# One-hot rows of a gate matrix: weight and comparison in one step on VectorE or ScalarE

## The chip, the cores and the metric

The kernel runs on one core of a Trainium2 chip. The time is the device time of one execution of the whole program, in microseconds (us). Before the change the median of three runs was 4549.05 us (4546.78 to 4557.33); the execution that was profiled took 4552.61 us.

## The reference

One layer of a hybrid decoder step for 512 prompt tokens and 32 sample tokens (544 in all, model width 2048). The part that matters here is its last one, the PEER channel mixer: every token picks, for 8 heads, 16 of 16384 one-neuron experts, and gets

```
e   = chosen expert ids (i1 * 128 + i2), 8 heads x 16 per token
g   = softmax(scores of the chosen)
act = gelu(peer_u[e] . x)
out = sum over the chosen of  g * act * peer_v[e]
```

So each token has 128 pairs (expert id, weight). The ids split into a row number i1 and a column number i2, both from 0 to 127.

## The kernel before

The 544 tokens are computed in two ways. 192 of them gather their expert rows one by one with indirect DMAs (the "rows" of line 1081, 384 of them, multiplied into accumulators on VectorE at lines 1129 and 1137). These run in the background, each tied to a matmul of the foreground by a dependency, so that they keep the pace of TensorE. The other 352 tokens take the dense way: TensorE multiplies all 16384 experts with the 352 tokens (`up`, 128 blocks of 128 experts), the result goes through gelu and is multiplied with a dense gate matrix G[expert, token], which is zero nearly everywhere; `down` multiplies that with all of `peer_v`.

`gate_matrix` (lines 1206 to 1255) builds G. It runs as a background task beside some 22 of the `up` blocks in the foreground. The tokens come in 4 tiles of up to 128; for each tile, three 128x128 matrices (i1, i2 and the weights) are transposed on TensorE and copied out of PSUM by ScalarE (lines 1218 to 1223; tiles `Ti1`, `Ti2`, `Tgv`, printed as `Ti` and `Tgv`). After that a partition is one of the 128 picks of a token, and a column is a token. Then, for four tokens at a time (a "quad", 88 in all, 8 to a group of 32 tokens):

- line 1244: VectorE makes `o2`, the one-hot of i2: a 128x512 comparison of a row of 0..127 with the column of each token, spread out;
- line 1246: VectorE makes `o1`, the one-hot of i1, in the same way;
- line 1247: GpSimd multiplies `o1` by the weights;
- line 1234 (`products`, two quads later): TensorE multiplies `o2` and `o1` token by token into one PSUM bank, which is the 128x128 gate matrix of each of the four tokens;
- line 1235: ScalarE copies the bank into `gs`, 32 tokens of which are written to DRAM by line 1255.

The foreground shares these engines. For every half of an `up` block (a "stream", 1024 columns of weights, 24 matmuls of line 258) ScalarE casts the weights to a rounded high part (`hi`, line 219) and VectorE subtracts it to get the low part (`lo`, line 220); at the end of a block VectorE scales the result (line 1198) and ScalarE applies gelu (line 1199).

What sets the order: every engine works its own list in order, and the lists are fixed when the program is built. Background tasks advance by one `yield` at a time; here by 2.8 steps per stream (`bg2.rate = 2.8`, line 1275). Casts and subtractions of the streams have a higher priority. Buffers limit the run ahead: 3 of `o1`, 3 of `o2`, 2 PSUM banks for the products, 3 of `hi` and `lo`.

Of the kernel before, what the change touches and what calls it, by code (L numbers as in the profile page):

```python
# [8 lines left out]
F = mybir.dt.float32  # L9
# [3 lines left out]
AF = mybir.ActivationFunctionType  # L13
OP = mybir.AluOpType
# [159 lines left out]
def program(tc, ins, outs):  # L174
    nc = tc.nc
    es = ExitStack()

    def pool(name, stack, bufs=1, **k):
        if k.get("space") is None:
            k["reuse_waits"] = "tile"  # L180
        return stack.enter_context(tc.tile_pool(name=name, bufs=bufs, **k))
# [20 lines left out]
    iota = cst[:, C_IOTA:C_IOTA + 128]  # L202
# [110 lines left out]
    p = ps_w.tile([128, 512], F, name="w1")  # L313
# [25 lines left out]
    for c in range(0, 8, 2):  # L339
        bg.rate = 1.6 if c > 2 else 0.4  # L340
        p = ps_mm.tile([128, 2, 512], F, name="mm")
# [6 lines left out]
    for ch in range(2):  # L348
        p = ps_mm.tile([128, 2, 512], F, name="mm")
# [23 lines left out]
    bias = [caus] + [ap.tile([128, (qb + 1) * 128], F, name=f"bias{qb}") for qb in range(1, 4)]  # L373
# [149 lines left out]
    for qb in range(1, 4):  # L523
        p = ps_w.tile([128, 512], F, name="w1")
# [4 lines left out]
    p = ps_w.tile([128, 512], F, name="w1")  # L529
# [94 lines left out]
    for n in range(2):  # L624
        s = staged(CH_V + n)
        p = ps_w.tile([128, 512], F, name="w1")
# [3 lines left out]
        p = ps_w.tile([128, 512], F, name="w1")  # L630
# [575 lines left out]
    def gate_matrix(t, groups, g0):  # L1206

        e1 = ra.tile([128, 128], I32, name="e1")
        nc.vector.tensor_copy(e1, ev[:, t])
        nc.vector.tensor_scalar(e1, e1, 7, None, op0=OP.arith_shift_right)  # L1210
        f1 = ra.tile([128, 128], F, name="f1")
        nc.vector.tensor_copy(f1, e1)
        f2 = ra.tile([128, 128], F, name="f2")
        nc.vector.scalar_tensor_tensor(f2, f1, -128.0, ev[:, t], op0=OP.mult, op1=OP.add)
        yield
        yield
        tr = []
        for nm, src in (("i1", f1), ("i2", f2), ("gv", gw[:, t])):
            p = ps_w.tile([128, 512], F, name="w1")
            nc.tensor.transpose(p[:, :128], src, ident)  # L1220
            d_ = ra.tile([128, 128], F, name="T" + nm)
            nc.scalar.copy(d_, p[:, :128])
            tr.append(d_)
        yield
        yield

        def wide(v, tk):
            return v[:, tk:tk + 4, None].to_broadcast([128, 4, 128])

        io = iota[:, None, :].to_broadcast([128, 4, 128])  # L1230
        def products(gs, q, o1, o2):
            p = ps_w.tile([128, 512], F, name="w1")
            for j in range(4):
                nc.tensor.matmul(p[:, j * 128:(j + 1) * 128], o2[:, j], o1[:, j], start=True, stop=True)
            nc.scalar.copy(gs[:, :, q * 4:q * 4 + 4].rearrange("p i t -> p t i"),
                           p.rearrange("p (t i) -> p t i", t=4))

        for i, tg in enumerate(groups):
            gs = ra.tile([128, 128, 32], F, name="gs", bufs=2)
            waiting = []  # L1240
            for q in range(8):
                tk = tg * 32 + q * 4
                o2 = ra.tile([128, 4, 128], F, name="o2", bufs=3)
                nc.vector.tensor_tensor(o2, io, wide(tr[1], tk), op=OP.is_equal)
                o1 = ra.tile([128, 4, 128], F, name="o1", bufs=3)
                nc.vector.tensor_tensor(o1, io, wide(tr[0], tk), op=OP.is_equal)
                nc.gpsimd.tensor_tensor(o1, o1, wide(tr[2], tk), op=OP.mult)
                waiting.append((q, o1, o2))
                if len(waiting) > 2:
                    products(gs, *waiting.pop(0))  # L1250
                yield
            for w in waiting:
                products(gs, *w)
                yield
            nc.sync.dma_start(g_dram[g0 + i], gs)
# [9 lines left out]
    while bg.queue:  # L1265
# [5 lines left out]
    ra = pool("ra", ras)  # L1271
    n1 = N1 // 32
    bg2.add(gate_matrix(1, range(4 - n1, 4), 0), gate_matrix(2, range(4), n1), gate_matrix(3, range(4), n1 + 4),
            gate_matrix(4, (0,), n1 + 8))
    bg2.rate = 2.8
    bg3.rate = 0.3
# [114 lines left out]
```

## Time and profile before

| | before |
|---|---|
| median of 3 runs | 4549.05 us |
| profiled execution | 4552.61 us |
| its span in the trace | 4550.8 us |
| TensorE busy | 4336.5 us (95%) |
| VectorE busy | 3281.7 us (72%) |
| ScalarE busy | 1728.2 us (38%) |
| GpSimd busy | 1277.5 us (28%) |

The profile shows one execution. PE is TensorE (PEld its weight load), DVE is VectorE, ACT is ScalarE, POOL is GpSimd, SP the engine that issues most DMAs. A busy share is an average over stages that differ: the gate matrix is built in one stretch of 278 us, from 2521.7 to 2799.5 us, and what counts for the change is read there. Busy time is the union of the instructions' times; instructions of one engine overlap at their ends, so what one costs its engine is the distance from its start to the next one's start, which is shorter than its duration.

### The profile page before, as it was taken

The page shows a single profiled execution, that of the slowest core. Times are in us where ns is not written, and L with a number is a line of the kernel's source. Part 1 is how long each engine was busy: PE and PEld are TensorE (multiplying, and loading weights), DVE is VectorE, ACT ScalarE, POOL GpSimd, SP SyncE. Part 2 cuts the span into 40 slices and gives each one's busy share as a digit, 9 for nine tenths or more (in the row PEclk, how much of TensorE's full clock was granted, in tenths as well). Part 3 has the DMA queues.
Part 4 walks back from the last instruction along what each step waited for, and adds up shares of the span by engine and source line. Part 5 has one row for each costly group of instructions (what it writes and reads, how often), then busy time and mean ns, then how long its engine had stood idle before and what let it go on. Part 6 is the DMA issues. An engine that isn't in the chain of part 4 may idle for free. (4 is left out here: it accounts for less than half of the span.)

```text
span 4550.8 us, 73815 instructions
## 1 busy us (share of the span) xinstructions
PE 4336.5 (95%) x29249; PEld 4147.9 (91%) x29249; DVE 3281.7 (72%) x4788; ACT 1728.2 (38%) x2374; POOL 1277.5 (28%) x1160
## 2 busy tenths in 40 slices
PE   8999989999999999999989899899999999999998
PEld 7976878699999889998988899898999999999998
DVE  6334735344556877778788997788888886888886
ACT  6232227454344434344323554322333333333333
POOL 3001011400001332333233563232343321343323
PEclk9999999999999999999999999999999999999999
DMA  8423443356657559989755567888999988999994
GB/s 267 165 85 115 142 131 109 118 159 185 185 177 213 161 181 333 326 317 320 255 171 173 197 234 281 318 325 323 338 336 345 352 312 276 348 346 348 346 352 167
DMA packets 342442, 1118.53 MB, mean 246 GB/s; under 512 B 42640, under 2 KB 137744, under 8 KB 289360
## 3 DMA queue, kind: packets, MB, share of 16 engines
q1 hardware_dynamic: 282704, 700.65, 46.1%
q0 software_dynamic: 59392, 413.17, 24.5%
q8 instruction: 229, 3.75, 0.3%
q14 instruction: 117, 0.96, 0.1%
HBM read 1050.75 MB, written 62.87 MB: 245 GB/s over the span
## 5 line engine op out<-in xcount | busy, mean ns | idle before, releaser
L219 ACT CAST hi<-raw 128x1024 fp32r<-128x1024 f32 x1050 | 1100.6, 1049 | 1918.2 <-PE mm L258 782.2
L220 DVE TENSOR_TENSOR lo<-raw,hi 128x1024 fp32r<-128x1024 f32 x1050 | 1322.9, 1262 | 614.7 <-ACT hi L219 590.1
L258 PE MATMUL mm<-xgd,hi 128*128 128x352 f32 (+1 forms) x4608 | 1116.9, 325 | 5.4 <-ACT hi L219 5.4
L258 PEld LDWEIGHTS mm<-xgd,hi 128*128 128x128 f32 x4608 | 806.5, 191 | 9.4 <-ACT hi L219 6.3
L258 PE MATMUL mm<-xgd,lo 128*128 128x352 f32 (+1 forms) x2304 | 750.0, 326 | 33.3 <-DVE lo L220 33.2
L258 PE MATMUL mm<-xF,hi 128*128 128x272 f32 x2976 | 702.2, 295 | 1.8 <-issue 1.1
L258 PE MATMUL mm<-xA,hi 128*128 128x272 f32 x2976 | 692.7, 292 | 1.3 <-ACT hi L219 1.0
L1318 PE MATMUL mm<-zh,hi 128*128 128x352 f32 x2048 | 664.6, 326 | 21.8 <-ACT zh L219 19.6
L1318 PE MATMUL mm<-zh,lo 128*128 128x352 f32 x2048 | 664.7, 325 | 4.4 <-DVE lo L220 4.2
L1318 PE MATMUL mm<-zl,hi 128*128 128x352 f32 x2048 | 665.6, 325 | 2.9 <-DVE zl L220 2.9
L258 PEld LDWEIGHTS mm<-xF,hi 128*128 128x128 f32 x2976 | 514.9, 189 | 39.0 <-issue 36.0
L1081 POOL DMA_INDIRECT row<-in_un,idx x192 | 333.5, 1737 | 707.8 <-PE mm L258 248.8
L258 PEld LDWEIGHTS mm<-xA,hi 128*128 128x128 f32 x2976 | 519.1, 191 | 10.2 <-issue 6.6
L1081 POOL DMA_INDIRECT row<-in_vn,idx x192 | 345.9, 1801 | 646.7 <-PE mm L1318 218.4
L258 PEld LDWEIGHTS mm<-xgd,lo 128*128 128x128 f32 x2304 | 438.2, 190 | 40.3 <-DVE lo L220 40.0
L1129 DVE SCALAR_TENSOR_TENSOR row<-row,xnat 128x2048 f32<-128x2048 f32 x192 | 440.6, 2295 | 47.1 <-DMA row<-in_un,idx 14.9
L258 PE MATMUL mm<-xA,lo 128*128 128x272 f32 x1488 | 438.5, 295 | 25.9 <-DVE lo L220 25.3
L1137 DVE SCALAR_TENSOR_TENSOR gacc<-row,hv,gacc 128x2048 f32<-128x2048 f32 x190 | 449.1, 2364 | 19.4 <-PE mm L1318 10.1
L258 PE MATMUL mm<-xF,lo 128*128 128x272 f32 x1488 | 432.4, 291 | 0.0
L1318 PEld LDWEIGHTS mm<-zh,hi 128*128 128x128 f32 x2048 | 388.0, 190 | 25.0 <-ACT zh L219 21.3
L1318 PEld LDWEIGHTS mm<-zh,lo 128*128 128x128 f32 x2048 | 388.4, 190 | 6.7 <-DVE lo L220 6.7
L1318 PEld LDWEIGHTS mm<-zl,hi 128*128 128x128 f32 x2048 | 388.6, 190 | 4.3 <-DVE zl L220 4.1
(362 smaller groups left out, 6272.1 us busy)
## 6 DMA issues: line engine op xcount, KB each, us to landing
raw<-in_u SPq DMA_DIRECT2D x256, 512.0 KB
raw<-in_v SPq DMA_DIRECT2D x256, 512.0 KB
raw<-in_w_gate SPq DMA_DIRECT2D x192, 512.0 KB
raw<-in_w_br SPq DMA_DIRECT2D x96, 512.0 KB
raw<-in_w_in SPq DMA_DIRECT2D x90, 512.0 KB
raw<-in_w_o SPq DMA_DIRECT2D x64, 512.0 KB
raw<-in_w_pq SPq DMA_DIRECT2D x64, 512.0 KB
g_dram<-gs SPq DMA_DIRECT2D x11, 2048.0 KB
```

Of the source, the lines that this page charges most:

```text
L219: nc.scalar.copy(hi, src)
L220: eng.tensor_tensor(lo, src, hi.bitcast(F), op=OP.subtract)
L258: last["mm"] = nc.tensor.matmul(p[:, i, :n], a[:, s], chunk(b[which], u + k), start=(u + k == 0 and pr == 0), stop=(u + k == k_chunks - 1 ...
L1081: i = nc.gpsimd.indirect_dma_start(out=r, out_offset=None, in_=ins[table], in_offset=bass.IndirectOffsetOnAxis(ap=ind[:, s:s + 1], axis=0))
L1129: j = nc.vector.scalar_tensor_tensor(r, r, 1.0, xn, op0=OP.mult, op1=OP.mult, accum_out=h)
L1137: j = nc.vector.scalar_tensor_tensor(acc, r, h, acc, op0=OP.mult, op1=OP.add)
L1318: last["mm"] = nc.tensor.matmul(p[:, 0, :NTA], a[:, s], b, start=(k == 0 and pr == 0), stop=(k == 7 and pr == 2))
```

## The change

`o1` is made in one step per token, with the row number and the weight of the token as per-partition numbers (a column of the transposed matrices). For tokens 0 and 1 of a quad VectorE does one 128x128 `tensor_scalar` each: compare, then multiply. For tokens 2 and 3 ScalarE does two 128x128 activations each: `Abs(iota - i1)`, and then `Relu(w - w * that)`, which is the weight where the number is hit and zero elsewhere. For this ScalarE also writes negated copies of the transposed i1 and weights (`N` + name), two per tile. GpSimd's multiply is gone. `o2` stays as it was.

```diff
-        tr = []
+        tr, neg = [], []
         for nm, src in (("i1", f1), ("i2", f2), ("gv", gw[:, t])):
             p = ps_w.tile([128, 512], F, name="w1")
             nc.tensor.transpose(p[:, :128], src, ident)
             d_ = ra.tile([128, 128], F, name="T" + nm)
             nc.scalar.copy(d_, p[:, :128])
             tr.append(d_)
+            if nm != "i2":
+                m_ = ra.tile([128, 128], F, name="N" + nm)
+                nc.scalar.mul(m_, p[:, :128], -1.0)
+                neg.append(m_)
...
                 o1 = ra.tile([128, 4, 128], F, name="o1", bufs=3)
-                nc.vector.tensor_tensor(o1, io, wide(tr[0], tk), op=OP.is_equal)
-                nc.gpsimd.tensor_tensor(o1, o1, wide(tr[2], tk), op=OP.mult)
+                for j in range(4):
+                    c = slice(tk + j, tk + j + 1)
+                    if j < 2:
+                        nc.vector.tensor_scalar(o1[:, j], iota, tr[0][:, c], tr[2][:, c], op0=OP.is_equal, op1=OP.mult)
+                    else:
+                        ab = ra.tile([128, 128], F, name="ab", bufs=2)
+                        nc.scalar.activation(ab, iota, AF.Abs, bias=neg[0][:, c])
+                        nc.scalar.activation(o1[:, j], ab, AF.Relu, bias=tr[2][:, c], scale=neg[1][:, c])
```

The lists of the engines in the second group of the first tile, before and after. ScalarE's list before (`gs<-w` is the copy of a quad's products, `hi<-raw` the cast of a stream, `ge<-ge` the gelu):

```order
L1235 COPY gs<-w_26659 128x4x128
L219 CAST hi<-raw 128x1024
L1199 ACTIVATE ge<-ge 128x352
L1235 COPY gs<-w_26690 128x4x128
L1235 COPY gs<-w_26710 128x4x128
L1235 COPY gs<-w_26730 128x4x128
L219 CAST hi<-raw 128x1024
L1235 COPY gs<-w_26756 128x4x128
```

ScalarE's list in the changed kernel, from the copy of the same quad (`ab<-cst,Ni` is an Abs, `o<-ab,Tgv,Ngv` a Relu):

```order
L1239 COPY gs<-w_26729 128x4x128
L1259 ACTIVATE o_26757<-ab,Tgv,Ngv 128x128
L219 CAST hi<-raw 128x1024
L1199 ACTIVATE ge<-ge 128x352
L1259 ACTIVATE o_26757<-ab,Tgv,Ngv 128x128
L1239 COPY gs<-w_26766 128x4x128
L1258 ACTIVATE ab<-cst,Ni_26382 128x128 x2
L1259 ACTIVATE o_26783<-ab,Tgv,Ngv 128x128 x2
L1258 ACTIVATE ab<-cst,Ni_26382 128x128
L1239 COPY gs<-w_26792 128x4x128
```

Two Abs and two Relu now stand between the copies of neighbouring quads. They belong to quads that TensorE multiplies two or three quads later, and the casts of the streams stand among them.

VectorE's list at the same place before (two 128x512 comparisons per quad):

```order
L220 TENSOR_TENSOR lo<-raw,hi 128x1024
L1244 TENSOR_TENSOR o_26629<-cst,Ti_26384 128x512
L1246 TENSOR_TENSOR o_26631<-cst,Ti_26380 128x512
L1244 TENSOR_TENSOR o_26643<-cst,Ti_26384 128x512
L1246 TENSOR_TENSOR o_26645<-cst,Ti_26380 128x512
```

And in the changed kernel:

```order
L220 TENSOR_TENSOR lo<-raw,hi 128x1024
L1248 TENSOR_TENSOR o_26681<-cst,Ti_26386 128x512
L1255 TENSOR_SCALAR o_26683<-cst,Ti_26380,Tgv 128x128 x2
L1248 TENSOR_TENSOR o_26701<-cst,Ti_26386 128x512
L1255 TENSOR_SCALAR o_26703<-cst,Ti_26380,Tgv 128x128 x2
```

The second comparison of a quad is replaced by two short instructions. TensorE's list has the same instructions in the same order in both kernels; GpSimd's list loses its 88 multiplies and keeps the row gathers.

## Rows read from the trace of the kernel before

**Rows 1.** Stretches: length; busy us (instructions) PE, PEld, DVE, ACT, POOL; PEclk; DMA; GB/s

```profile
2521.70:2799.50 277.80, 259.90 (x1760) 250.70 (x1761) 264.87 (x277) 149.22 (x165) 160.22 (x101) 0.99 0.62 223
2800.00:2830.00 30.00, 30.00 (x186) 30.00 (x185) 17.63 (x19) 10.31 (x14) 2.76 (x2) 1.00 1.02 355
2830.00:3000.00 170.00, 157.73 (x951) 156.11 (x951) 132.64 (x148) 51.59 (x64) 39.87 (x25) 0.95 0.91 332
```

**Rows 2.** Waits, 2521.7 to 2799.5: waiter <- releaser: total us, times, longest

```profile
POOL o L1247 <- DVE o L1246: 88.5, 67, 7.7
ACT gs L1235 <- PE w L1234: 67.7, 57, 2.8
ACT ge L1199 <- DVE ge L1198: 30.1, 20, 3.4
...
PE w L1234 <- POOL o L1247: 17.5, 22, 1.8
...
ACT Ti L1222 <- PE w L1220: 8.2, 4, 3.6
```

**Rows 3.** Groups by shape, same stretch: count | busy us, mean ns | idle before

```profile
L258 PE MATMUL mm<-xgd,hi 128*128 128x352 f32 x696 | 178.3, 338 | 0.0
L1247 POOL TENSOR_TENSOR o<-o,Tgv 128x512 f32<-128x512 f32 x88 | 133.8, 1520 | 113.9 <-DVE o L1246 88.5 <-ACT Tgv L1222 8.5 <-PE mm L258 7.7
...
L258 PE MATMUL mm<-xgd,lo 128*128 128x352 f32 x348 | 113.5, 326 | 0.0
L1246 DVE TENSOR_TENSOR o<-cst,Ti 128x512 f32<-128x512 f32 x88 | 96.9, 1102 | 0.0
...
L1244 DVE TENSOR_TENSOR o<-cst,Ti 128x512 f32<-128x512 f32 x88 | 73.5, 836 | 1.0 <-ACT Ti L1222 1.0
...
L219 ACT CAST hi<-raw 128x1024 fp32r<-128x1024 f32 x43 | 45.6, 1060 | 22.5 <-PE mm L258 15.1 <-issue 6.9 <-ACT Tgv L1222 0.5
...
L1199 ACT ACTIVATE ge<-ge 128x352 f32<-128x352 f32 x22 | 10.9, 497 | 30.1 <-DVE ge L1198 30.1
```

**Rows 4.** Timeline of DVE: start us, duration us, instruction

```profile
2643.09 0.68 DVE L1244 TENSOR_TENSOR o<-cst,Ti 128x512 f32<-128x512 f32 x1
2643.70 1.53 DVE L1246 TENSOR_TENSOR o<-cst,Ti 128x512 f32<-128x512 f32 x1
2645.14 0.68 DVE L1244 TENSOR_TENSOR o<-cst,Ti 128x512 f32<-128x512 f32 x1
```

**Rows 5.** Timeline of PE: one quad's products and the next

```profile
2641.46 1.05 PE L1234 MATMUL w<-o,o 128*128 128x128 f32 x8
...
2643.32 0.49 PE L258 MATMUL mm<-xgd,hi 128*128 128x352 f32 x2
...
2643.81 1.05 PE L1234 MATMUL w<-o,o 128*128 128x128 f32 x8
```

**Rows 6.** Timeline of ACT: instructions that follow each other without a wait

```profile
2509.40 0.40 ACT L1020 ACTIVATE gw<-gw,rsN 128x128 f32<-128x128 f32 x1
2509.71 1.03 ACT L219 CAST hi<-raw 128x1024 fp32r<-128x1024 f32 x1
2510.65 0.40 ACT L1020 ACTIVATE gw<-gw,rsN 128x128 f32<-128x128 f32 x1
...
2644.90 1.12 ACT L1235 COPY gs<-w 128x512 f32<-128x512 f32 x1 [1.23 <-PE w L1234]
2645.79 1.08 ACT L219 CAST hi<-raw 128x1024 fp32r<-128x1024 f32 x1
```

**Rows 7.** Groups by shape, whole span: an activation without a per-partition number

```profile
L288 ACT ACTIVATE fq<-xnat 128x128 f32<-128x128 f32 x15 | 4.3, 306 | 3.9 <-POOL fs L289 2.0 <-DVE xnat L1145 1.9
```

**Rows 8.** Groups by shape, whole span: VectorE's tensor_scalar with one and two numbers

```profile
L422 DVE TENSOR_SCALAR mex<-mex,sm 128x256 f32<-128x256 f32 x16 | 5.6, 353 | 0.6
...
L424 DVE TENSOR_SCALAR mex<-mex,sm,c 128x256 f32<-128x256 f32 x8 | 3.3, 410 | 0.2
...
L422 DVE TENSOR_SCALAR ex<-ex,sm 128x128 f32<-128x128 f32 x8 | 2.5, 308 | 0.2
```

## The prediction

> **What bounds the kernel now.** I read the stretches first. The gate matrix is built from 2521.7 to 2799.5 us, and there VectorE is busy for 264.9 of 277.8 us (95%), TensorE for 259.9, ScalarE for only 149.2 [rows 1]. So in this stretch VectorE is the engine with least air, although over the whole span it is at 72%. The reader should not take TensorE's 259.9 for work that has to be done: a busy matmul is counted with its whole duration, and the next one starts before it ends. What TensorE needs is read from starts. A quad's products and the nine stream matmuls behind them take 2643.81 - 2641.46 = 2.35 us, and three stream matmuls 2643.81 - 2643.32 = 0.49, so 0.163 each [rows 5]. The stretch holds 696 + 348 = 1044 stream matmuls [rows 3] and 88 quads: 88 x 2.35 = 206.8 us take 792 of them along, the other 252 cost 41.1, and twelve transposes some 0.2 each (2.4, my guess). The granted clock was 0.99 of full speed there [rows 1], 1% of the stretch or 2.8 us. TensorE's need is 253.1 us. It takes 277.8, so about 25 us are lost.
>
> The waits name the loss: TensorE waits for the weighted one-hot of GpSimd for 17.5 us in 22 places, and GpSimd for VectorE's comparison for 88.5 us in 67 places [rows 2]. (Refilling the matmul pipe after these waits makes up most of the remainder; that is my reading.) GpSimd itself is not full: its multiply is busy 133.8 us [rows 3]. So the chain is VectorE, GpSimd, TensorE, and VectorE is late. Why it is late stands in the timeline: the same 128x512 comparison takes 0.68 us in one place and 1.53 in the next [rows 4], with 1.102 and 0.836 as the means of the two lines [rows 3]. The long ones are those beside a multiply of GpSimd, I take it. Against 0.68 the 176 comparisons lose 96.9 + 73.5 - 176 x 0.68 = 50.7 us.
>
> **The change, engine by engine.**
>
> GpSimd: 88 multiplies go (133.8 us busy, [rows 3]). Nothing waits for GpSimd any more but the row gathers, which keep their order and their tie to TensorE's matmuls.
>
> VectorE: 88 comparisons of `o1` go, and 176 `tensor_scalar` of 128x128 with two per-partition numbers come. No row has that form. With one number and 128x128 it takes 308 ns; a second number took 410 - 353 = 57 ns more at 128x256 [rows 8]. So 0.31 to 0.37 us, I take 0.365: 64 us. The 88 comparisons of `o2` cost 0.68 without the neighbour: 60 us. The rest of its work was 264.9 - 96.9 - 73.5 = 94.5 us [rows 1, 3]. Together 219 us at most, against TensorE's 253: VectorE is no longer the engine with least air. That cover is worth about 34 us.
>
> ScalarE: this is where the price stands. It keeps 88 copies of products at 2645.79 - 2644.90 = 0.89 us each (start to start, [rows 6]): 78.3 us; 44 casts (43 and a cut one, [rows 3]) at 2510.65 - 2509.71 = 0.94 [rows 6]: 41.4; 22 gelus at 0.50 [rows 3]: 11.0; and twelve copies of transposes, to which eight negated ones are added, at about 0.25, 5.0 in all. That is 135.7 us. It gets 176 Abs with one per-partition number and 176 Relu with two. An activation of 128x128 with one such number keeps the engine for 2509.71 - 2509.40 = 0.31 us [rows 6]: Abs costs 54.6 us. With two numbers no row exists. Below: the second is free, 0.31, 54.6 us. Above: the second costs what the first does. The first costs 402 - 306 = 0.10 us, by the 0.40 of the activation in [rows 6] and the 306 ns of one without [rows 7]; so 0.41, 72.2 us. I take the upper end, because it is the only price of such a number that the trace shows. ScalarE then needs 135.7 + 54.6 + 72.2 = 262.5 us; with the lower end 244.9.
>
> The Trainium skill has a price for this. "ScalarE: Activation LUTs", section "What ACT_TABLE_LOAD costs", says that an activation takes 186 ns plus 0.833 ns per element, that every per-partition operand adds about 93 ns, and that neighbours overlap by about 93 ns. The trace agrees where it can be read: 0.10 for one such operand, 0.31 from start to start. It speaks for my upper end; by it Abs would cost 0.294 and Relu 0.387 (estimates worked out from that page), ScalarE 7 us less in the stretch, and the time 7 us less than my forecast.
>
> No activation table is loaded for the change: the lists have the same number of loads in both kernels. DMA does not change, save that weights stream in faster: 0.62 of the DMA engines' time in this stretch [rows 1] becomes 0.65.
>
> **The sum.** TensorE needs 253, ScalarE 262.5, VectorE 219. So the stretch is taken over by ScalarE, by a small margin, and its length is ScalarE's work plus the waits that it can't avoid. Today it waits 67.7 us for products, 30.1 for the scaling before gelu and 8.2 for the transposes [rows 2]. An engine that is behind finds its inputs ready, so most of this goes; I keep the transposes' waits less the first, 8.2 - 3.6 = 4.6 us, and nothing else. That makes 267 us. 277.8 - 267 = 11 us less. Is it given back? Right behind the stretch TensorE is busy without a gap for 30 us, with DMA at 1.02, and then for 157.7 of 170 us with DMA at 0.91 [rows 1]. These transfers (the accumulator, the gelu results, the gate matrix) are started when the gate matrix's buffers are released, so they move forward with its end: I count no loss. The profiled execution took 4552.6 us, 3.6 more than the median; 4552.6 - 11 = 4541.6, and against the median 4549.05 - 11 = 4538 us.
>
> **Rivals.**
>
> TensorE bounds it: the second number on a Relu is free, ScalarE needs 245, and the stretch is TensorE's 253 plus the 4.6 around the transposes, 258: 20 us less, 4529 us. For it: waiting behind the products is all that holds TensorE today. Against it: the price of the first number.
>
> Two full queues in lockstep: ScalarE and TensorE are both at 95% and more, work in fixed order, and have two PSUM banks between them. VectorE reached 95% under such conditions [rows 1]; 262.5 / 0.95 = 276 us: 1.5 us less, 4547 us, no change that can be seen. For it: the casts of the streams come in lumps of 0.94 us and the gelu waits for VectorE. Against it: most of ScalarE's new work is needed only two quads (some 5 us) later, so small delays are taken up.
>
> ScalarE becomes a brake, and the kernel slower. Mechanism: an Abs and the Relu on it are dependent instructions of one engine, and `ab` has two buffers, so each waits for one that stands one or two places ahead. If the waits take away the overlap of neighbours, Abs and Relu cost their full durations, 0.40 and 0.50: 2 x 0.90 = 1.80 us per quad instead of 1.44, 158 us instead of 127. ScalarE then needs 294 us, with the 4.6 it is 299: 21 us more, 4570 us. It decides from 1.56 us per quad on, since 135.7 + 4.6 + 88 x 1.56 is 277.8. For it: there is only 8% between 1.44 and that. Against it: in the list most pairs stand two apart, and the distance of two starts (0.7 us) is longer than one duration.
>
> Hidden anyway: the gate matrix is finished earlier, but the DMA-bound stretch behind it gives the time back. Then 4549 us. For it: DMA at 1.02 and 0.91 behind it [rows 1]. Against it: nothing of that traffic could have been on its way before.
>
> **How the numbers follow.** A difference of under 0.2% (9.1 us, so 4540 to 4558) can't be told from no change in this kernel's runs. Chances: forecast 0.43, of which a quarter falls inside that band because 11 us is near its edge; TensorE bounds it 0.22; lockstep 0.15; brake 0.14; given back 0.06. Faster is 0.32 + 0.22 = 0.54. Same is 0.11 + 0.15 + 0.06 and a third of the brake, 0.04, that is 0.36. Slower is 0.10. The range goes from a little below the TensorE case (4526, the loss of 25 us gone nearly whole) up to the middle between no change and the brake, 4556. The forecast's own range is 4532 to 4544.
>
> **What would show it.** In the changed profile the stretch should be 262 to 270 us long; VectorE's comparison at 0.68 throughout and VectorE busy for about 210 us; ScalarE busy for over 90% of the stretch; TensorE's waits for GpSimd gone, and what waits remain there should be for ScalarE's `o1` or for its copies. Starts of Relu 0.41 apart would confirm the price; 0.31 would mean the first rival, 0.50 the brake. It would be wrong if TensorE waits 20 us or more for ScalarE, if the casts of the streams come late, or if the stretch shrinks by more than 10 us and the time does not.

## The result and the profile after

The changed kernel takes 4527.31 us (median of 5 runs, 4518.91 to 4529.82) against 4549.05 before: ratio 0.9941, interval 0.9918 to 0.9964. By this ratio, which is not the quotient of the two medians, it is 26.8 us less (16 to 37); the medians themselves lie 21.7 us apart. 11 were forecast. The direction was right and the median lies in the range, near its lower end, but the saving is two to two and a half times the forecast. The profiled execution has a span of 4528.0 us.

The stretches of the changed kernel that answer to [rows 1]: from the first transpose to the last quad's products, the 30 us behind it, and the DMA-bound stretch after that.

```profile
2537.10:2795.60 258.50, 254.46 (x1759) 252.49 (x1760) 193.75 (x366) 250.91 (x525) 25.05 (x13) 0.98 0.65 236
2796.00:2826.00 30.00, 30.00 (x186) 30.00 (x185) 16.35 (x17) 10.42 (x14) 2.73 (x2) 1.00 1.03 367
2826.00:3000.00 174.00, 164.63 (x997) 161.71 (x996) 140.46 (x161) 53.13 (x66) 43.11 (x27) 0.98 0.96 350
```

The gate stretch is 19.3 us shorter (277.8 to 258.5). VectorE went from 264.9 busy us to 193.8, ScalarE from 149.2 to 250.9: it is at 97% of the stretch, and TensorE at 98%. The waits of the same stretch, which answer to [rows 2]:

```profile
DVE lo L220 <- ACT hi L219: 50.3, 32, 3.3
...
ACT Ti L1222 <- PE w L1220: 6.6, 3, 3.6
...
PE w L1238 <- DVE o L1255: 3.8, 3, 2.1
...
ACT ge L1199 <- DVE ge L1198: 1.2, 2, 0.9
...
ACT gs L1239 <- PE w L1238: 1.0, 1, 1.0
```

TensorE's wait for a weighted one-hot fell from 17.5 to 3.8 us, and ScalarE's waits for products and gelu inputs (67.7 and 30.1) to 1.0 and 1.2: an engine that is behind finds its inputs ready. A new line stands on top: VectorE waits 50.3 us for the casts of ScalarE. The groups of this stretch, for [rows 3]:

```profile
L258 PE MATMUL mm<-xgd,hi 128*128 128x352 f32 x695 | 178.8, 339 | 0.0
...
L1259 ACT ACTIVATE o<-ab,Tgv,Ngv 128x128 f32<-128x128 f32 x176 | 80.9, 493 | 0.1
...
L1258 ACT ACTIVATE ab<-cst,Ni 128x128 f32<-128x128 f32 x176 | 63.2, 402 | 0.4
L1248 DVE TENSOR_TENSOR o<-cst,Ti 128x512 f32<-128x512 f32 x88 | 60.4, 686 | 3.8 <-PE w L1238 3.7
...
L1255 DVE TENSOR_SCALAR o<-cst,Ti,Tgv 128x128 f32<-128x128 f32 x176 | 53.2, 343 | 0.0
```

The comparison is at 0.686 us in the mean, without the long ones of [rows 4]; `tensor_scalar` with two numbers takes 0.343. The Relu lasts 0.493, the Abs 0.402. What they cost ScalarE is read from their starts, in its timeline (answers to [rows 6]):

```profile
2641.66 0.47 ACT L1259 ACTIVATE o<-ab,Tgv,Ngv 128x128 f32<-128x128 f32 x1
2642.04 0.68 ACT L1258 ACTIVATE ab<-cst,Ni 128x128 f32<-128x128 f32 x2
2642.63 0.48 ACT L1259 ACTIVATE o<-ab,Tgv,Ngv 128x128 f32<-128x128 f32 x1
2643.14 0.40 ACT L1258 ACTIVATE ab<-cst,Ni 128x128 f32<-128x128 f32 x1
...
2653.38 0.49 ACT L1199 ACTIVATE ge<-ge 128x352 f32<-128x352 f32 x1
2653.78 0.48 ACT L1259 ACTIVATE o<-ab,Tgv,Ngv 128x128 f32<-128x128 f32 x1
2654.17 1.11 ACT L1239 COPY gs<-w 128x512 f32<-128x512 f32 x1
2655.05 0.68 ACT L1258 ACTIVATE ab<-cst,Ni 128x128 f32<-128x128 f32 x2
```

A Relu takes 0.38 us (2641.66 to 2642.04), two Abs 0.59, so 0.295 each, a gelu 0.40, a copy of products 0.88 (2654.17 to 2655.05). One kind of pair costs more: where an Abs stands right behind a Relu after two Abs before it (2642.63 to 2643.14), it starts 0.51 us after the Relu. By the program's order it writes the `ab` buffer that this Relu has just read; there are two of them. This is so in 11 places of the stretch.

### The profile page after: what moved, and what is told of

It is laid out like the page before. It is cut to its first block, busy times and chain, and to the rows that moved or that the text cites. A ratio compares the mean times of both kernels' runs of the same rounds, so it can differ in the third digit from the quotient of the medians.

```text
span 4528.0 us, 74125 instructions
## 1 busy us (share of the span) xinstructions
PE 4332.8 (96%) x29249; PEld 4148.1 (92%) x29249; DVE 3210.0 (71%) x4876; ACT 1829.0 (40%) x2734; POOL 1160.5 (26%) x1072
## 4 chain that ended last, share of the span: by engine, by line
PE 72%; DVE 9%; DMA 8%; ACT 4%; issue 4%; POOL 3%; another core or an unknown queue 0%; SPq 0%; DVEq 0%; ACTq 0%; POOLq 0%
PE mm L258 44%; PE mm L1330 20%; DVE lo L220 4%; DMA raw<-in_w_gate 3%; DMA raw<-in_u 1%; ACT hi L219 1%; PE mm L359 1%; POOL eq L1007 1%; DMA gl<-ge_dram 1%; PE w L545 1%; ACT gs L1239 1%; POOL cand L993 1%; DVE gacc L1137 1%; DMA raw<-in_w_br 1%; PE w L1238 1%
## 5 line engine op out<-in xcount | busy, mean ns | idle before, releaser
L1081 POOL DMA_INDIRECT row<-in_un,idx x192 | 342.8, 1786 | 844.2 <-PE mm L258 326.7
L1129 DVE SCALAR_TENSOR_TENSOR row<-row,xnat 128x2048 f32<-128x2048 f32 x192 | 440.1, 2292 | 42.7 <-PE mm L1330 12.8
```

The source lines that it names most:

```text
L1081: i = nc.gpsimd.indirect_dma_start(out=r, out_offset=None, in_=ins[table], in_offset=bass.IndirectOffsetOnAxis(ap=ind[:, s:s + 1], axis=0))
L1129: j = nc.vector.scalar_tensor_tensor(r, r, 1.0, xn, op0=OP.mult, op1=OP.mult, accum_out=h)
```

## The experiments

A run's ratio is to the kernel before, timed on the same chip. Every profile was cut at the same five places, so that a gain can be put where it arises. "Gate stretch" is as above; "DMA-bound stretch" goes from the first product of `down` to the first use of a gelu result that stayed on the chip (block 50). "Rest" ends with the last products of `down`; the 21 us of a span behind them are in no column. There is one profile for each line. Lengths in us:

| kernel | ratio (interval) | ahead | gate stretch | DMA-bound stretch | rest |
|---|---|---|---|---|---|
| before | 1 | 2521.8 | 277.7 | 424.0 | 1240.0 |
| control, before | 1.0002 (0.9987-1.0017) | 2495.6 | 277.7 | 428.2 | 1243.1 |
| control 2, before | one run | 2496.8 | 277.8 | 415.1 | 1238.9 |
| changed | 0.9941 (0.9918-0.9964) | 2537.2 | 258.4 | 406.9 | 1237.6 |
| control, changed | 0.9943 (0.9922-0.9965) | 2542.5 | 258.4 | 412.6 | 1241.8 |
| control 2, changed | one run | 2504.2 | 256.4 | 416.8 | 1241.9 |
| no multiply | 0.9923 (0.9898-0.9947) | 2505.5 | 250.2 | 412.8 | 1234.6 |
| Relu with one number | 0.9937 (0.9914-0.9960) | 2499.7 | 250.2 | 420.4 | 1237.8 |
| idle GpSimd multiply added | 0.9981 (0.9966-0.9996) | 2505.6 | 271.2 | 404.9 | 1239.4 |
| three tokens on VectorE | 0.9923 (0.9896-0.9949) | 2538.7 | 250.1 | 408.2 | 1239.4 |
| the same again | 0.9931 (0.9911-0.9951) | 2509.2 | 250.8 | 420.2 | 1236.6 |
| four on VectorE | 0.9934 (0.9914-0.9953) | 2537.7 | 252.3 | 415.7 | 1238.1 |
| one on VectorE | 1.0055 (1.0035-1.0076) | 2535.4 | 324.4 | 430.5 | 1234.4 |
| before, six gelu buffers | 0.9983 (0.9967-0.9999) | 2501.0 | 277.7 | 399.6 | 1244.7 |

Between the gate stretch and the first `down` product lie another 62 to 69 us (24 with one token on VectorE, where the `up` blocks that usually stand there had already run beside the gate matrix).

**Is GpSimd's multiply what made VectorE late?** In the kernel before, the multiply is taken out:

```diff
-                nc.gpsimd.tensor_tensor(o1, o1, wide(tr[2], tk), op=OP.mult)
```

> The kernel before without GpSimd's multiply; o1 stays unweighted, so the weights are left out of the gate matrix. Theory A (the comparisons were long because GpSimd's multiply ran beside them, and VectorE was late for that reason): all 176 comparisons take 0.68 us, VectorE is busy for about 214 us of the stretch, and the stretch falls from 278 to TensorE's 253 plus 5, about 258, the same as in the changed kernel, although ScalarE does nothing new. Theory B (the long comparisons have another cause, and the gain came from halving VectorE's share of the one-hot): comparisons stay at 0.84 and 1.10 in the mean, and the stretch stays above 270.

Its gate stretch and its two comparisons:

```profile
2505.50:2755.70 250.20, 250.12 (x1760) 250.02 (x1761) 202.66 (x277) 150.35 (x165) 30.77 (x13) 0.99 0.70 250
```

```profile
L1244 DVE TENSOR_TENSOR o<-cst,Ti 128x512 f32<-128x512 f32 x88 | 60.2, 686 | 13.6 <-PE w L1234 12.6 <-ACT Ti L1222 0.7
L1246 DVE TENSOR_TENSOR o<-cst,Ti 128x512 f32<-128x512 f32 x88 | 60.0, 683 | 0.0
```

All 176 comparisons are short, VectorE needs 202.7 us, and TensorE is busy for 250.12 of 250.20 us: it never waits. The long comparisons did come from the multiply: theory A stands, although it expected a stretch of 258. And this is TensorE's real need, 250.2 against the 253.1 of the prediction. The run takes out two things at once, though: what the multiply does to VectorE beside it, and GpSimd's step between VectorE and TensorE. The next run has the first alone. The largest gain that any change of the one-hot can bring here is 277.7 - 250.2 = 27.5 us; the changed kernel has 19.3 of it.

**Does contention alone bring the loss back?** To the changed kernel a multiply of GpSimd is added whose result nobody reads:

```diff
+                dm = ra.tile([128, 4, 128], F, name="dm", bufs=2)
+                nc.gpsimd.tensor_tensor(dm, o2, wide(tr[2], tk), op=OP.mult)
```

> The changed kernel with a GpSimd multiply of 128x512 per quad added, which reads o2 and writes a tile that nobody reads. By theory A VectorE's two-input comparisons get long again where they lie beside it (mean above 0.9 us instead of 0.685), VectorE's busy time in the stretch rises from 194 to 230 to 260 us, and the stretch comes out at 258 to 270 us: much of the loss of before returns only if VectorE passes TensorE's 253. By theory B the comparisons stay at 0.685 and the stretch at 258.

```profile
L1255 DVE TENSOR_SCALAR o<-cst,Ti,Tgv 128x128 f32<-128x128 f32 x176 | 117.3, 703 | 0.0
L1261 POOL TENSOR_TENSOR dm<-o,Tgv 128x512 f32<-128x512 f32 x88 | 104.4, 1187 | 131.8 <-DVE o L1248 115.5 <-ACT ab L1258 16.2
...
L1248 DVE TENSOR_TENSOR o<-cst,Ti 128x512 f32<-128x512 f32 x88 | 59.8, 679 | 0.0
```

The stretch goes from 258.4 back to 271.2 us, with VectorE at 254.3 busy us. So a multiply that no instruction waits for costs 12.8 us by running beside VectorE, a little more than the 258 to 270 us expected. The instruction that pays was not the one expected: the comparison stays at 0.679, and `tensor_scalar` doubles to 0.703, since GpSimd starts when `o2` is ready and then meets VectorE's next instruction. Which of the two pays is seen in the timeline of this run, VectorE's lines and GpSimd's:

```profile
2645.81 1.34 DVE L1255 TENSOR_SCALAR o<-cst,Ti,Tgv 128x128 f32<-128x128 f32 x2
2646.03 1.04 POOL L1261 TENSOR_TENSOR dm<-o,Tgv 128x512 f32<-128x512 f32 x1 [0.83 <-DVE o L1248]
...
2647.80 1.22 DVE L220 TENSOR_TENSOR lo<-raw,hi 128x1024 fp32r<-128x1024 f32 x1
2647.90 2.03 POOL L1261 TENSOR_TENSOR dm<-o,Tgv 128x512 f32<-128x512 f32 x1 [0.82 <-DVE o L1248]
```

The multiply starts before the second `tensor_scalar` of the first pair, which ends only behind it, and the two last 1.34 us together. The second multiply starts 0.10 us behind a subtraction: there the subtraction keeps its 1.22 us and the multiply grows to 2.03.

**Which engine bounds the changed kernel?** The Relu's scale becomes a constant:

```diff
-                        nc.scalar.activation(o1[:, j], ab, AF.Relu, bias=tr[2][:, c], scale=neg[1][:, c])
+                        nc.scalar.activation(o1[:, j], ab, AF.Relu, bias=tr[2][:, c], scale=-1.0)
```

> The changed kernel with the Relu's scale as the constant -1 and not as a per-partition number; the weights come out wrong for tokens 2 and 3 of a quad. Price: Relu from start to start falls from 0.385 to 0.30 us, ScalarE's busy time in the stretch from 251 to about 236. If TensorE bounds the stretch (need 253), it stays at 256 to 259. If ScalarE does, with TensorE waiting in small pieces, it falls by several us, to 250 to 254.

One remark in that text is mistaken: the weights are results of a softmax and so at most 1, thus weight minus distance is never positive off the hit, and nothing of the computation is lost. Its gate stretch, and its Relu:

```profile
2499.70:2749.90 250.20, 250.14 (x1760) 250.04 (x1761) 195.01 (x365) 235.95 (x525) 37.12 (x13) 0.99 0.68 244
```

```profile
L1259 ACT ACTIVATE o<-ab,Tgv 128x128 f32<-128x128 f32 x176 | 62.5, 403 | 0.0
```

The second number costs 493 - 403 = 90 ns. With 15 us less on ScalarE the stretch falls by 8.2 us to TensorE's floor: the second answer of the expectation. So ScalarE at 97% did cost the changed kernel 8 us, although TensorE was busy for 254.5 of 258.5 us as well. The time of the whole program does not show them (ratio 0.9937 against 0.9941).

**Moving tokens between the engines.** The limit in `if j < 2` becomes 3, 4 and 1:

```diff
-                    if j < 2:
+                    if j < 3:
```

> The changed kernel with three tokens of a quad on VectorE and one on ScalarE. From measured starts (Abs 0.295, Relu 0.385, tensor_scalar 0.27 us) ScalarE's need falls from 251 to 191 us and VectorE's rises from 194 to 217. If a full ScalarE holds up casts and through them VectorE, which costs the changed kernel 8 us over the 250.2 us of the kernel without weights, the gate stretch falls to 250 to 251 us with TensorE never idle. If those 8 us are the start of the stretch (clock and first transposes), it stays at 256 to 258.

```profile
2538.70:2788.80 250.10, 250.06 (x1760) 249.96 (x1761) 215.90 (x453) 205.80 (x350) 37.87 (x13) 0.99 0.69 246
```

With three tokens on VectorE both engines have air (86% and 82%) and TensorE never waits: 250.1 us, and 250.8 in a second profile. The pair named above is common here, since a quad has only one Abs: in 64 of 66 places where an Abs is right behind a Relu the overlap is gone, and the Relu costs some 0.52 us. The wait for casts, VectorE's largest in the changed kernel, falls from 50.3 to 16.9 us. A pair of the one kind, and the wait:

```profile
2602.10 0.49 ACT L1259 ACTIVATE o<-ab,Tgv,Ngv 128x128 f32<-128x128 f32 x1
2602.63 0.40 ACT L1258 ACTIVATE ab<-cst,Ni 128x128 f32<-128x128 f32 x1
```

```profile
DVE lo L220 <- ACT hi L219: 16.9, 22, 4.5
```

ScalarE has the air to pay for the lost overlap. The second profile was taken for this expectation:

> Three tokens on VectorE and one on ScalarE once more, as the version to keep: gate stretch 250.1 us with TensorE never idle, 8 us less than the changed kernel; ratio to before 0.992.

The ratios, 0.9923 and 0.9931, lie better than the changed kernel's 0.9941 and 0.9943, but the intervals overlap: the 8 us are shown by the stretch, not by the time of the whole program. With four tokens on VectorE:

> All four tokens on VectorE, none on ScalarE. VectorE's need is about 241 us, ScalarE's 131. TensorE bounds it: 250 to 256 us. If VectorE holds up TensorE whenever it passes 95% of the stretch, as in the kernel before, 253 to 258.

```profile
2537.70:2790.00 252.30, 251.85 (x1760) 250.60 (x1761) 235.90 (x541) 151.57 (x174) 27.11 (x13) 0.99 0.68 244
```

VectorE is at 93% and the stretch is 2.2 us longer than with three tokens. TensorE's waits for VectorE's one-hot make only 0.5 us of that, and profiles of one kernel differ by up to 2 us in this stretch, so what the fuller VectorE costs stays open. With one:

> One token on VectorE, three on ScalarE: ScalarE gets 88 Abs and 88 Relu more, 88 x 0.68 = 60 us on 251. ScalarE then bounds the stretch clearly: 311 us of work plus some 7 of waits, 318 us, about 60 us slower than the changed kernel. If the price per token were the 0.31 + 0.41 of the prediction it would be 63 us more; if dependent pairs lost their overlap (0.40 + 0.50), 79 us more and 337.

```profile
2535.40:2859.80 324.40, 314.22 (x2005) 287.63 (x2006) 196.82 (x295) 320.62 (x715) 31.18 (x16) 0.99 0.62 217
```

ScalarE is busy for 320.6 of 324.4 us and bounds the stretch, as the brake would, but from the amount of work and not from lost overlap: two Relu take 0.77 us from start to next start.

```profile
2652.21 0.87 ACT L1259 ACTIVATE o<-ab,Tgv,Ngv 128x128 f32<-128x128 f32 x2
2652.98 0.39 ACT L1258 ACTIVATE ab<-cst,Ni 128x128 f32<-128x128 f32 x1
```

The stretch is 6 us longer than expected. It also holds more of the foreground: 53 casts and 27 gelus where the changed kernel has 43 and 22, some 11 us of ScalarE's time. The whole program loses less than the 66 us of the stretch, because TensorE gets through 245 more matmuls in it which otherwise come behind it.

**Where do the other microseconds come from?** The changed kernel's first profile was also 17 us shorter in the DMA-bound stretch and 15 longer ahead of the gate matrix, where its work is the same. The controls:

> The kernel before once more, as a control. Gate stretch (first transpose to last quad's products) 278 us by every theory. For the rest of the span two theories differ: if the 17 us that the changed kernel's profile was shorter in the DMA-bound stretch behind the gate matrix (first down product to the first gate product of block 50: 424 before, 407 after) are scatter from run to run, this control shows some other length there, anywhere from 405 to 430, and the stretches ahead of the gate matrix scatter by 5 to 15 us too; if the change causes them, it shows 424 within 3.

> The changed kernel once more, as a control and with more rounds. The gate stretch should be 258 us as in its first profile. If the time moved by the gate stretch alone (277.7 to 258.4, 19 us), the ratio is 0.9957 within its interval; if 17 us more are saved in the DMA-bound stretch behind it, the ratio is 0.992 and that stretch is 407 us again.

> The kernel before, a third profile, on the same chip as the next ones. Gate stretch 277.7 us. For the DMA-bound stretch (first down product to the first gate product of block 50), so far 424 and 428 us before and 407 and 413 after: if the difference belongs to the kernels, 420 to 430 here; if it is scatter, anything from 405.

> The changed kernel, a third profile, same chip. Gate stretch 258.4 us. DMA-bound stretch: 405 to 415 us if the difference belongs to the kernels; if it is scatter, up to 430. Ahead of the gate matrix the two kernels have the same work: a difference of over 10 us there is scatter.

The gate stretch repeats within 0.1 us before and within 2 us after (258.4, 258.4 and 256.4). The DMA-bound stretch was 424, 428 and 415 us before and 407, 413 and 417 after, so the two overlap; ahead of the gate matrix the lengths differ by up to 38 us for one and the same kernel (2504.2 to 2542.5, on different chips). The second controls ran on one chip: there the gate stretch is 21.4 us shorter, the DMA-bound stretch 1.7 longer, and the whole span 11.3 shorter (4515.8 and 4504.5). A last run lets the gelu results be fetched earlier in the kernel before:

```diff
-GL = 4
+GL = 6
```

> The kernel before with six buffers, and not four, for the gelu results that are read back in the DMA-bound stretch, so that their loads are issued earlier. Gate stretch 277.7 us, nothing is changed there. If TensorE loses the 12 to 15 us of the DMA-bound stretch because single loads land late there (a wait of 7.5 us for one of them in both profiles of before, 1.4 in the changed kernel), the stretch falls to 405 to 415 us. If bandwidth is what is short, it stays at 420 to 430.

The stretch falls to 399.6 us in this one profile, the shortest of all and 15.5 below the kernel before on the same chip, with the gate stretch untouched. So that stretch depends on when its loads are issued, and can move by some 15 us without the gate matrix.

## Why the prediction was wrong

The failed step is a term of the sum: ScalarE's need, put at 262.5 us, from which the length of the stretch (267) was taken. ScalarE was busy for 250.9 us, 11.6 less. Its unavoidable waits, the other term, were 7.6 us and not 4.6, so that the stretch is 258.4 us long.

- Relu: 0.41 us forecast, 0.38 measured: 66.9 us and not 72.2. The upper end was the right end (the second number costs 90 ns like the first), but it was made from a single start distance (0.31) and a difference of durations rounded up to 0.10. By the Trainium skill ("ScalarE: Activation LUTs", "What ACT_TABLE_LOAD costs") the estimate came to 0.387, and that of Abs to 0.294; the trace has 0.38 and 0.295, so the page was nearer than my rows.
- Abs: 0.295 for 0.31, 51.9 us for 54.6. Gelu: 0.40 from start to start, where the duration of 0.50 was taken: 8.8 us for 11.0. Copies: about 0.87 for 0.89, 1.8 us less. With the Relu's 5.3 us these make 12.0 of less work; the busy time is 11.6 less.
- TensorE's need: 253.1 forecast, 250.1 to 250.8 where it never waits.
- VectorE: "219 at most" was safe; it is 193.8. That its long comparisons come from GpSimd's multiply was argued in the prediction; it is now shown from both sides, by removing the multiply (comparisons at 0.68, 278 to 250 us) and by adding an idle one (258 to 271). The 12.8 us of the second are VectorE's contention alone, in a kernel whose ScalarE is full; how the 27.5 of the first divide between contention and GpSimd's own step was not tried.
- "An engine that is behind finds its inputs ready": right for the products and the gelu inputs (67.7 and 30.1 us fell to 1.0 and 1.2). For the transposes 3.0 us are left without the first wait, where 4.6 were kept; the waits that the sum left out lie at the start of the stretch and at its end.
- The brake's lost overlap: it exists, but only where a Relu and the Abs that takes its buffer are neighbours, in 11 places of the changed kernel at some 0.13 us each.
- No loss behind the stretch: right for the 30 us behind it, in which TensorE is busy throughout, as before.

The mechanism of the sum held: ScalarE's work and the waits that it can't avoid make the stretch. Of its 7.6 idle us, 2.6 lie in the first 5.4 us. In the next 214.3 it is busy for 213.2:

```profile
2542.50:2756.80 214.30, 210.42 (x1478) 208.50 (x1477) 161.83 (x308) 213.22 (x444) 19.02 (x11) 1.00 0.66 237
```

The other 3.9 come in the last 39 us, behind the longest wait of TensorE. Where ScalarE has 15 or 45 us less to do, the stretch ends at TensorE's 250. The number of the first rival (TensorE bounds it, 258 us, 4529 us) came true by luck: the second number is not free, and TensorE's own floor is 250 us, not 258. The lockstep (276 us) did not come: ScalarE reached 97% of the stretch and TensorE 98%.

How ScalarE holds up TensorE was not foreseen. The prediction expected TensorE to wait for ScalarE's one-hots or copies; late casts stand in it only among the signs of being wrong. VectorE's timeline in the changed kernel shows another way:

```profile
2658.59 0.34 DVE L1255 TENSOR_SCALAR o<-cst,Ti,Tgv 128x128 f32<-128x128 f32 x1
2660.02 1.23 DVE L220 TENSOR_TENSOR lo<-raw,hi 128x1024 fp32r<-128x1024 f32 x1 [1.09 <-ACT hi L219]
2661.17 0.34 DVE L1255 TENSOR_SCALAR o<-cst,Ti,Tgv 128x128 f32<-128x128 f32 x1
```

The subtraction of a stream waits 1.09 us for ScalarE's cast, and the second `tensor_scalar` of a quad, which is ready, stands behind it until 2661.17. So the lateness of a full ScalarE comes to TensorE under VectorE's name. VectorE waits 50.3 us for casts in 32 places; TensorE waits 3.8 us for VectorE's one-hot in three. Two of these three stand behind such a wait of VectorE, and in both a row accumulation of 2.3 us (lines 1129 and 1137) is in VectorE's list too, as it is in the runs in which TensorE never waits; the third, 0.50 us, has no wait for a cast near it. The longest is 2.09 us, VectorE's lines and TensorE's:

```profile
2752.17 1.23 DVE L220 TENSOR_TENSOR lo<-raw,hi 128x1024 fp32r<-128x1024 f32 x1 [2.19 <-ACT hi L219]
2753.31 2.35 DVE L1137 SCALAR_TENSOR_TENSOR gacc<-row,hv,gacc 128x2048 f32<-128x2048 f32 x1
2755.57 0.69 DVE L1248 TENSOR_TENSOR o<-cst,Ti 128x512 f32<-128x512 f32 x1
2756.18 0.60 DVE L1255 TENSOR_SCALAR o<-cst,Ti,Tgv 128x128 f32<-128x128 f32 x2
...
2756.64 1.34 PEld L1238 LDWEIGHTS w<-o,o 128*128 128x128 f32 x8 [2.35 <-issue]
2756.67 1.61 PE L1238 MATMUL w<-o,o 128*128 128x128 f32 x8 [2.09 <-DVE o L1255]
...
2757.93 0.93 PE L258 MATMUL mm<-xgd,hi 128*128 128x352 f32 x2
...
2760.65 1.05 PE L1238 MATMUL w<-o,o 128*128 128x128 f32 x8
```

Behind it the granted clock falls to about half, the lower level of 1.2 GHz. The quad's products and the nine stream matmuls take 2760.65 - 2756.67 = 3.98 us instead of 2.35 [rows 5]. The stretch from 2757.0 to 2760.2 (0.52 granted), and the one at the same place in the third profile of the changed kernel, where TensorE has waited 2.05 us and the clock stays up (1.00):

```profile
2757.00:2760.20 3.20, 3.20 (x16) 3.20 (x15) 3.20 (x7) 2.35 (x6) 0.00 (x0) 0.52 0.94 402
```

```profile
2723.00:2726.20 3.20, 3.15 (x23) 2.96 (x24) 3.20 (x7) 2.29 (x6) 0.00 (x0) 1.00 1.04 445
```

That profile has the gate stretch of 256.4 us, 6.2 above TensorE's floor. In the first profile the waits (3.8) and the low clock (1.6) make 5.4 of the 8.2 us. How the rest splits up was not tried.

Of the measured 26.8 us (16 to 37), 19.3 are shown in the gate stretch (8.3 more than the forecast, from these two terms of ScalarE). The remaining 7.5, for which the sum has no term, are less than the interval's half width; of the medians' 21.7 us only 2.4 remain. Whether some of it belongs to the change, by way of the DMA-bound stretch, stays open: three profiles of each kernel overlap there.

## What to carry to other kernels

Before an engine's work is handed to another, sum the second one's list by start-to-start distances of each form, and ask what stands behind that engine's output: here, at 97%, it showed up as a wait of VectorE for casts, and behind that as a wait of TensorE for VectorE. A helper on GpSimd can be paid for twice, by its own time and by the instructions that VectorE runs beside it. Between engines that share a job, look for a split that leaves each some air: here three tokens to one (VectorE 86%, ScalarE 82%) reached TensorE's floor, as did the changed kernel once ScalarE was at 94%.

## What the runs showed of the hardware

A GpSimd multiply that no instruction waits for doubled VectorE's `tensor_scalar` (0.343 to 0.703 us in the mean) and left the 128x512 comparison, which had ended before it began, at 0.68. The Trainium skill ("SBUF — State Buffer", "Who interferes with whom") says that issue order decides who blocks; the rows agree, with a `tensor_scalar` that ends behind the multiply and a multiply that lasts 2.03 us behind a subtraction. The Abs and the Relu on it, dependent instructions of one engine two places apart, lost none of the overlap of neighbours: 0.295 and 0.38 us from start to start at durations of 0.40 and 0.49. Directly behind one another the overlap was gone: an Abs behind the Relu that had just read its buffer started 0.51 to 0.53 us after it, where a copy behind a Relu started after 0.39. That the buffer is the cause is read from the order of the list; no run changed the number of buffers.
